# Two splits ahead of the last up block's evacuation, and a pair's sums due one weight later, in a hybrid encoder block

## The chip, the core and the metric

The kernel runs on one core of a Trainium2 chip. The metric is the device time of one execution, in microseconds (us); lower is better. Before the change it was 694.92 us, the median of three runs (694.84 to 695.49).

## What is computed

One layer of an encoder on 512 positions of width 1024, in float32. The part that matters here is the channel mixer at its end, FFN_HIDDEN = 2816 wide:

```python
h = rms_norm(x, norm_ffn_g[l])
up = causal_dwconv(h @ w_up[l], conv_ffn_w[l])
a, b = jnp.split(up, 2, axis=-1)
x = x + (jax.nn.silu(a) * b) @ w_down[l]
return rms_norm(x, norm_f_g)
```

The layer's first half (short convolution, forgetting attention, gates and merge) lies ahead of it and is not touched.

## The kernel before

**Layout.** Positions lie along the free axis, channels in 22 blocks of 128 on the partitions. Block j of the hidden layer has two column blocks of w_up, its a half (weight `up2j`) and its b half (`up2j+1`). The mixer has two phases (L43): blocks 0 to 11 with their share of w_down, then blocks 12 to 21 with the rest. A phase is an *up stage* followed by a *down stage*.

**Weights in two parts.** Every product is made from high and low parts: `wh*xh + wl*xh + wh*xl`, three float32r matmuls of 128x128 by 256 columns. So each weight that comes from memory is *split* before use (`split`, L253): ACT copies it into `wh` (L275), DVE subtracts that copy from the raw weight into `wl` (L279). `wh` and `wl` have two buffers each: a weight can be split once the weight two places before it is done on PE. A split also issues the load of a weight some places ahead on SP, and it then runs some of the planner's list (below).

**Seven products.** The down stages, and the up stages of blocks 1, 2, 5, 14 and 16 (`SUP`, L61), use a Strassen-like scheme: a two by two block product in seven products instead of eight (`seven`, L824). A step there has two weights, P (three products of each of two doubles: 18 matmuls) and F (four: 24 matmuls). An ordinary up weight has 48 matmuls. The names used below: the first down stage begins with P18, F18, P19, F19; block 14 uses P30, F30, P31, F31; the second down stage begins with P34, F34 and P35, and its fourth step is P37. Blocks 15, 17, 18, 19 and 20 have the weights up30/31, up34/35, up36/37, up38/39 and up40/41. Within a P or F all `wh` matmuls stand first, then those with `wl`; of an ordinary up weight the first eight matmuls use `wh` alone.

**Evacuation of an up block** (`up`, L1141). For each half: DVE multiplies the bank with the norm's scale (`mul`, L1171), ACT and DVE make the three taps of the convolution (`taps`: ACT L566, DVE L567 and L570). Behind the second half comes the gating (`glu`, L1227): ACT's SiLU (L1231; in the last block a table load for the coming square root, L1233, too) and a product of the halves. For an even j it is `ge` on GpSimd (POOL, L1236), for an odd one `go` (L1243). Two gated blocks form a pair q = j // 2: their *sums* are four short DVE steps (t13 in L1253 and L1254, t24 in L1257 and L1258), and the values and sums are split like weights into `gh` (ACT, L1262) and `gl` (DVE, L1263), in four steps.

**The planner.** What isn't urgent goes into the list `later` as (due, cost, tags, function). `run_later` (L224) runs, at each split, what is due by that weight's number while a budget of microseconds lasts: 4.2 for an up weight, 1.6 for a P and 1.2 for an F while anything tagged "e" (an evacuation) is pending, and 1.7, 1.6 and 0.75 otherwise (L286, L288). It skips what is not due and stops at the first due step that doesn't fit. Steps run in this way are queued behind the split's own copy and subtraction on their engines (`after_split`, L159). A pair's sums and splits are put in front of the "e" steps. After a seven-product block, its merge (nine steps) is tagged "e", and the evacuations of the blocks behind it are tagged so as well until the list is empty of them; otherwise an evacuation is issued at once. `glu` of an odd block first runs all that is left of earlier pairs (`flush_only`, L1238), because `go` has one buffer.

A pair's dues count from k, the number of the weight last split when `glu` runs: L1268.

```python
d = (2, 3, 4) if j + 1 < PHASES[ph][1] else (4, 5, 6)
```

The sums are due at k + d[0], two of the four splits at k + d[1] and two at k + d[2]. For the last block of a phase `go` itself is put off too, to k + 3, on DVE.

**Order on the engines.** PE's order is the code's. On ACT and DVE the tile framework, when it builds the program, puts the instructions in an order by its own estimate of when each is ready; among ready ones the code's order decides. The order that it chose is what the trace shows.

Of the kernel before, what the change touches and what calls it, by code (L numbers as in the profile page):

```python
# [42 lines left out]
PHASES = ((0, 12), (12, NP))  # L43
# [17 lines left out]
SUP = ((1, 2, 5), (14, 16))  # L61
# [9 lines left out]
def block_kernel(ctx, tc, xT, vecs, wv, win, wmix, wo, wup, wst, wdp, outT):  # L71
# [10 lines left out]
    def keep(ins):  # L82
        return tc.keep_in_program_order(ins)
# [72 lines left out]
    later = []  # L156
    held = dict.fromkeys(NRAW, 0)

    def after_split():  # L159

        st = ExitStack()
        for ins in order.values():
            st.enter_context(tc.issue_after(ins))
        return st

    def tag_of(k):
        return "raw" if stream[k][0][0] != "F" else "rf" if k >= ff0 else "rg"

    def load(upto):
        for k in range(len(raws), min(upto, len(stream) - 1) + 1):  # L170
            nm, src, ncol = stream[k]
            tag = tag_of(k)
            if held[tag] == NRAW[tag] or tag not in pools:
                return
            held[tag] += 1
            raw = pools[tag].tile([P, D], F32, tag=tag, name=f"raw_{nm}", bufs=NRAW[tag])
            if k == 0:

                keep(nc.scalar.dma_start(raw[:, VB:ncol], src[:, VB:]))
                keep(nc.sync.dma_start(raw[:, :VB], src[:, :VB]))  # L180
            else:
                keep(nc.sync.dma_start(raw[:, :ncol], src if tag == "raw" else made[src]))
            raws.append(raw[:, :ncol])
# [40 lines left out]
    def run_later(k, us):  # L224

        n = 0
        while n < len(later):
            if later[n][0] <= k and later[n][1] <= us + 0.1:
                us -= later[n][1]
                with after_split():  # L230
                    later.pop(n)[3]()
            elif later[n][0] <= k:
                return
            else:
                n += 1
# [11 lines left out]
    def flush_only(tags):  # L247

        while n := [n for n, w in enumerate(later) if set(w[2]) & set(tags)]:
            with after_split():  # L250
                later.pop(n[0])[3]()

    def split(hl=None):  # L253

        k = len(parts)
        if k == len(stream):
            return
        nm, _, ncol = stream[k]
        load(k + (LOOK if len(raws) > KB else AHEAD))
        if hl is None:  # L260
            hl = []
            for x in "hl":
                if k == 0:
                    wp.tile([P, PADW[x]], F32, tag=f"pad{x}", name=f"pad_{x}")
                w0 = VOFF if k < KB else 0
                hl.append(wp.tile([P, D], F32R, tag=f"w{x}", name=f"w{x}_{nm}", bufs=2)[:, w0 : w0 + ncol])
        hi, lo = hl
        raw = raws[k]
        if k == 0:
            for cs in (slice(VB, S + H), slice(0, VB)):  # L270
                keep(nc.vector.tensor_copy(hi[:, cs], raw[:, cs]))
        elif k == 1:
            keep(nc.vector.tensor_copy(hi, raw))
        else:
            ins = nc.scalar.activation(hi, raw, AF.Copy)  # L275
            order["hi"] = ins.ins
            if k < KB:
                keep(ins)
        ins = nc.vector.tensor_sub(lo, raw, hi.bitcast(F32))  # L279
        order["lo"] = ins.ins  # L280
        if k < KB:
            keep(ins)
        held[tag_of(k)] -= 1
        parts.append((hi, lo))
        if any(("e",) in w[2] for w in later):
            run_later(k, {"u": 4.2, "P": 1.6, "F": 1.2}[nm[0]])  # L286
            return
        run_later(k, {"u": 1.7, "P": 1.6, "F": 0.75, "i": 3.0, "m": 3.0, "d": 0 if nm == "dp1" else 2.1}.get(nm[0], 3.5))  # L288
# [275 lines left out]
    def taps(u, z, w):  # L564

        nc.scalar.activation(u, z, AF.Copy, scale=col(w + 2))  # L566
        nc.vector.scalar_tensor_tensor(  # L567
            u[:, 1:], z[:, : S - 1], col(w + 1), u[:, 1:], op0=ALU.mult, op1=ALU.add
        )
        nc.vector.scalar_tensor_tensor(  # L570
            u[:, 2:], z[:, : S - 2], col(w), u[:, 2:], op0=ALU.mult, op1=ALU.add
        )
# [117 lines left out]
    z, e, o = (ap.tile([n, S], F32, tag="pp", name=nm, bufs=NPP) for nm in ("fz", "fe", "fo"))  # L690
# [104 lines left out]
    for i in range(n + LA):  # L795
# [8 lines left out]
        if 0 <= i - LA < n:  # L804
            pr, e, qb = units[i - LA]
# [335 lines left out]
    def up(j, ph, rb2, pu=None):  # L1141
        uu = []

        def tap(i, z):
            u = fp.tile([P, S], F32, tag="fu", name=f"fu{j}{i}", bufs=3)
            taps(u, z, CF + 3 * (2 * j + i))
            uu.append(u)

        if j in SUP[ph]:
            c = 2 * SUP[ph].index(j)  # L1150
            slot()
            seven(
                UPD[ph][c : c + 2], NU[ph] + c, {j: USETS[j]}, lambda q, g: up_form(ph, q, g), of="x",
                done=lambda i, banks, ids: merge(ph, j, banks, ids, rb2, tap, uu),
            )
            slot()
            return
        evacs = []
        for i in range(2):
            slot()  # L1160
            p = pu[i] if pu else block(f"up{2 * j + i}", x1h, x1l, True)
            if i and j + 1 == PHASES[ph][1]:
                split_next()
                if any(("e",) in w[2] for w in later):
                    flush_only((("e",),))
                    split()
            z = [None]

            def mul(i=i, p=p, z=z):
                z[0] = fp.tile([P, S], F32, tag="fz", name=f"fz{j}{i}", bufs=4)  # L1170
                nc.vector.tensor_mul(z[0], p, rb2)  # L1171

            evac = [(0.7, mul), (1.4, lambda i=i, z=z: tap(i, z[0]))]
            if i:
                evac.append((0, lambda: glu(ph, j, uu)))
            if any(("e",) in w[2] for w in later):
                later.extend((0, us, (("e",), acc.last) if x == 0 else (("e",),), f) for x, (us, f) in enumerate(evac))
            else:
                for _, f in evac:
                    f()  # L1180
# [46 lines left out]
    def glu(ph, j, uu):  # L1227
        a, b = uu
        q, k = j // 2, len(parts) - 1
        g0 = place(ph, q)  # L1230
        nc.scalar.activation(a, a, AF.Silu)  # L1231
        if j == NP - 1:
            nc.scalar.activation(tbl, a[: 4 * H, :1], AF.Sqrt, scale=0.0, bias=eps[: 4 * H])  # L1233
        if j % 2 == 0:
            ge = glu.even = fp.tile([P, 2, 2 * P], F32, tag="ge", name=f"ge{q}", bufs=2)
            keep(nc.gpsimd.tensor_mul(ge, a.rearrange(halves_of, h=2), b.rearrange(halves_of, h=2)))  # L1236
            return
        flush_only([("q", x) for x in range(q)])  # L1238
        ge = glu.even
        go = fp.tile([P, 6, 2 * P], F32, tag="gr", name=f"go{q}")  # L1240

        def mul(eng):
            return eng.tensor_mul(go[:, 0:2, :], a.rearrange(halves_of, h=2), b.rearrange(halves_of, h=2))  # L1243

        if j + 1 < PHASES[ph][1]:
            keep(mul(nc.gpsimd))
        else:
            later.append((k + 3, 0.7, (("q", q),), lambda: mul(nc.vector)))
        b11, b12 = ge[:, 0, :], ge[:, 1, :]
        b21, b22, t1, t2, t3, t4 = (go[:, i, :] for i in range(6))  # L1250

        def t13():
            nc.vector.tensor_sub(t1, b11, b12)  # L1253
            nc.vector.tensor_sub(t3, b22, b12)  # L1254

        def t24():
            nc.vector.scalar_tensor_tensor(t2, t1, -1.0, b22, op0=ALU.mult, op1=ALU.subtract)  # L1257
            nc.vector.scalar_tensor_tensor(t4, t2, -1.0, b21, op0=ALU.mult, op1=ALU.subtract)  # L1258

        def hl(src, gs):  # L1260
            def f():
                nc.scalar.activation(gh[:, gs, :], src, AF.Copy)  # L1262
                nc.vector.tensor_sub(gl[:, gs, :], src, gh.bitcast(F32)[:, gs, :])  # L1263

            return f


        d = (2, 3, 4) if j + 1 < PHASES[ph][1] else (4, 5, 6)  # L1268
        w = [(d[0], 0.85, t13), (d[0], 0.85, t24), (d[1], 0.7, hl(ge[:, : 1 + ph, :], slice(g0, g0 + 1 + NF * ph, NF)))]
        w += [(d[x > 0 and 2 or 1], 0.7, hl(go[:, x : x + 2, :], slice(g0 + 1 + x, g0 + 3 + x))) for x in (0, 4, 2)]  # L1270
        at = next((x for x, i in enumerate(later) if ("e",) in i[2]), len(later))
        later[at:at] = [(k + n, us, (("q", q),), f) for n, us, f in w]
# [264 lines left out]
```

## Time and profile before

| | |
|---|---|
| median of three runs | 694.92 us |
| profiled execution | 694.18 us |
| its span, first to last instruction | 692.4 us |
| granted TensorE clock, mean | 0.997 |
| ACT busy | 53% |
| POOL busy | 28% |
| largest wait of ACT's weight copies for PE, in total (wh_F) | 28.7 us |

Rows of the timeline are read so: start in us from the first instruction, duration in us, engine, line of the code, operation, out<-in by the program's names (numbers left out, so `wh_F` is the high part of any F weight), shapes, and a count where equal instructions follow each other; in brackets the time that the engine stood idle just before, and what ended it. PE's matmuls overlap, so their starts, not their ends, show its pace. Rows of the waits: engine, line, "<-" what it waited for, total us, times, longest.

### The profile page before, as it was taken

The page shows a single profiled execution, that of the slowest core. Times are in us where ns is not written, and L with a number is a line of the kernel's source. Part 1 is how long each engine was busy: PE and PEld are TensorE (multiplying, and loading weights), DVE is VectorE, ACT ScalarE, POOL GpSimd, SP SyncE. Part 2 cuts the span into 40 slices and gives each one's busy share as a digit, 9 for nine tenths or more (in the row PEclk, how much of TensorE's full clock was granted, in tenths as well). Part 3 has the DMA queues.
Part 4 walks back from the last instruction along what each step waited for, and adds up shares of the span by engine and source line. Part 5 has one row for each costly group of instructions (what it writes and reads, how often), then busy time and mean ns, then how long its engine had stood idle before and what let it go on. Part 6 is the DMA issues. An engine that isn't in the chain of part 4 may idle for free. (4 is left out here: it accounts for less than half of the span.)

```text
span 692.4 us, 14690 instructions
## 1 busy us (share of the span) xinstructions
PE 683.1 (99%) x5936; PEld 680.6 (98%) x5936; DVE 554.2 (80%) x858; ACT 368.3 (53%) x579; POOL 190.5 (28%) x201
## 2 busy tenths in 40 slices
PE   9999999999999999999999999999999999999996
PEld 9999999999999999999999999999999999999995
DVE  6677787877578778769879699998787899988894
ACT  5675755554554444546554555545444544545572
POOL 6134947542020201214400144340100325231000
PEclk9999999999999999999999999999999999999998
DMA  8629999552568586788998498888945996676413
GB/s 308 225 67 293 216 243 204 134 120 92 185 144 221 166 268 205 230 308 213 158 313 241 126 233 222 200 242 231 252 149 167 337 231 157 188 168 182 154 31 122
DMA packets 65012, 137.53 MB, mean 199 GB/s; under 512 B 5760, under 2 KB 30352, under 8 KB 64688
## 3 DMA queue, kind: packets, MB, share of 16 engines
q1 hardware_dynamic: 44664, 107.28, 47.2%
q0 software_dynamic: 18464, 26.03, 23.4%
q10 hardware_dynamic: 1816, 3.29, 1.3%
q8 instruction: 46, 0.75, 0.4%
q14 instruction: 22, 0.18, 0.1%
HBM read 132.31 MB, written 47.71 MB: 260 GB/s over the span
## 5 line engine op out<-in xcount | busy, mean ns | idle before, releaser
L211 POOL DMA_DIRECT2D f<-in_wst_dram x66 | 77.7, 1371 | 27.1 <-DMA f<-f 26.8
L309 PE MATMUL p_up<-x1h,wh_up 128*128 128x256 f32 x416 | 81.2, 276 | 0.0
L309 PE MATMUL p_up<-x1l,wh_up 128*128 128x256 f32 x416 | 81.0, 276 | 0.0
L309 PE MATMUL p_up<-x1h,wl_up 128*128 128x256 f32 x416 | 81.0, 276 | 0.0
L279 DVE TENSOR_TENSOR wl_F<-raw_F,wh_F 128x1024 fp32r<-128x1024 f32 (+1 forms) x42 | 55.9, 1330 | 20.0 <-ACT wh_F L275 20.0
L275 ACT ACTIVATE wh_F<-raw_F 128x1024 fp32r<-128x1024 f32 (+1 forms) x42 | 44.3, 1054 | 39.5 <-PE dn L327 28.7
L309 PEld LDWEIGHTS p_up<-x1h,wh_up 128*128 128x128 f32 x416 | 62.7, 188 | 0.0
L309 PEld LDWEIGHTS p_up<-x1l,wh_up 128*128 128x128 f32 x416 | 62.7, 188 | 0.0
L309 PEld LDWEIGHTS p_up<-x1h,wl_up 128*128 128x128 f32 x416 | 62.6, 188 | 0.0
L309 PE MATMUL p_in<-xgh,wh_in 128*128 128x256 f32 x288 | 56.8, 279 | 0.0
L309 PE MATMUL p_in<-xgh,wl_in 128*128 128x256 f32 x288 | 56.6, 278 | 0.0
L309 PE MATMUL p_in<-xgl,wh_in 128*128 128x256 f32 x288 | 56.5, 278 | 0.0
L279 DVE TENSOR_TENSOR wl_P<-raw_P,wh_P 128x768 fp32r<-128x768 f32 (+1 forms) x42 | 41.7, 992 | 14.7 <-ACT wh_P L275 8.6
L327 PE MATMUL dn<-gh,wh_F 128*128 128x256 f32 x216 | 51.2, 277 | 1.2 <-ACT wh_F L275 1.2
L275 ACT ACTIVATE wh_P<-raw_P 128x768 fp32r<-128x768 f32 (+1 forms) x42 | 35.1, 835 | 32.1 <-PE dn L327 23.2
L327 PE MATMUL dn<-gl,wh_F 128*128 128x256 f32 x216 | 51.0, 276 | 0.0
L1236 POOL TENSOR_TENSOR ge<-fu,fu 128x512 f32<-128x512 f32 x11 | 20.1, 1831 | 110.5 <-DVE fu L570 85.6
L279 DVE TENSOR_TENSOR wl_up<-raw_up,wh_up 128x1024 fp32r<-128x1024 f32 x34 | 43.8, 1288 | 7.4 <-ACT wh_up L275 7.4
L275 ACT ACTIVATE wh_up<-raw_up 128x1024 fp32r<-128x1024 f32 x34 | 35.8, 1054 | 19.4 <-PE p_up L309 9.3
L309 PEld LDWEIGHTS p_in<-xgh,wh_in 128*128 128x128 f32 x288 | 44.7, 188 | 0.7
L309 PEld LDWEIGHTS p_in<-xgl,wh_in 128*128 128x128 f32 x288 | 43.7, 188 | 0.0
L309 PEld LDWEIGHTS p_in<-xgh,wl_in 128*128 128x128 f32 x288 | 43.6, 188 | 0.0
(343 smaller groups left out, 2211.8 us busy)
## 6 DMA issues: line engine op xcount, KB each, us to landing
raw_F<-f SPq DMA_DIRECT2D x41, 512.0 KB, 5.7
raw_up<-in_wup_dram SPq DMA_DIRECT2D x34, 512.0 KB, 5.6
raw_P<-in_wst_dram SPq DMA_DIRECT2D x41, 384.0 KB, 5.4
raw_in<-in_win_dram SPq DMA_DIRECT2D x24, 512.0 KB, 3.6
f<-in_wst_dram POOLq DMA_DIRECT2D x41, 256.0 KB, 6.8
f<-in_wst_dram SPq DMA_DIRECT2D x20, 512.0 KB, 7.1
f<-in_wst_dram POOLq DMA_DIRECT2D x20, 512.0 KB, 9.1
f<-f SPq DMA_DIRECT2D x40, 256.0 KB, 6.5
```

The source lines that it names most:

```text
L211: return lambda: keep(nc.gpsimd.dma_start(dst, src, accum_op=ALU.add))
L275: ins = nc.scalar.activation(hi, raw, AF.Copy)
L279: ins = nc.vector.tensor_sub(lo, raw, hi.bitcast(F32))
L309: keep(nc.tensor.matmul(out[:, cs], w, x[:, cs], start=start and i == 0 and c == 0, stop=stop and i == 2 and c == len(cut) - 1,))
L327: keep(nc.tensor.matmul(out, wl if x == 1 else wh, xl if x == 2 else xh, start=opens and bk not in seen, stop=closes and bk not in left,))
L1236: keep(nc.gpsimd.tensor_mul(ge, a.rearrange(halves_of, h=2), b.rearrange(halves_of, h=2)))
```

## The change

In `up`, for the second half of the last block of a phase: before, one split followed by a second one only if an "e" step is pending, in which case these are run first. After, two splits in any case, and then the pending "e" steps. In `glu`, the dues of a pair whose next block is one of `SUP` (j = 1, 13 and 15) go from (2, 3, 4) to (3, 4, 5).

```diff
             if i and j + 1 == PHASES[ph][1]:
                 split_next()
-                if any(("e",) in w[2] for w in later):
-                    flush_only((("e",),))
-                    split()
+                split()
+                flush_only((("e",),))
...
-        d = (2, 3, 4) if j + 1 < PHASES[ph][1] else (4, 5, 6)
+        d = (4, 5, 6) if j + 1 == PHASES[ph][1] else (3, 4, 5) if j + 1 in SUP[ph] else (2, 3, 4)
```

Since the second split comes ahead of the last block's `glu`, k is one larger there, and with it the dues of that pair (q5 in the first phase, q10 in the second).

## The prediction

> **What bounds the kernel now.** I read the page's first lines, then the waits of PE, then PE's timeline around each wait.
>
> ```profile
> span 692.4 us, 14690 instructions
> PE 683.1 (99%) x5936; PEld 680.6 (98%) x5936; DVE 554.2 (80%) x858; ACT 368.3 (53%) x579; POOL 190.5 (28%) x201
> ```
>
> PE is the bound, so an edit counts only if it shortens or makes a hole in PE's row. The waits of PE name weight splits alone:
>
> ```profile
> PE dn L327 <- ACT wh_F L275: 1.2, 2, 0.7
> PE dn L327 <- DVE wl_F L279: 0.4, 1, 0.4
> ```
>
> The timeline shows four holes in the channel mixer:
>
> ```profile
> 467.13 0.84 PE L327 MATMUL dn<-gh,wl_P 128*128 128x256 f32 x6
> 468.62 0.38 PE L327 MATMUL dn<-gh,wh_F 128*128 128x256 f32 x1 [0.66 <-ACT wh_F L275]
> ```
>
> ```profile
> 554.09 0.28 PE L327 MATMUL dn<-gl,wh_F 128*128 128x256 f32 x1
> 554.72 0.38 PE L327 MATMUL dn<-x1h,wl_F 128*128 128x256 f32 x1 [0.35 <-DVE wl_F L279]
> ```
>
> ```profile
> 609.59 0.28 PE L327 MATMUL p_up<-x1l,wh_up 128*128 128x256 f32 x1
> 610.02 0.50 PE L327 MATMUL p_up<-x1h,wl_up 128*128 128x256 f32 x2 [0.15 <-DVE wl_up L279]
> ```
>
> ```profile
> 632.55 0.73 PE L327 MATMUL dn<-gh,wl_P 128*128 128x256 f32 x5
> 633.78 0.38 PE L327 MATMUL dn<-gh,wh_F 128*128 128x256 f32 x1 [0.50 <-ACT wh_F L275]
> ```
>
> Six matmuls last 0.84 us with the last one's 0.28, so starts are 0.113 us apart ((0.84 - 0.28) / 5). The last of the six starts at 467.70; the next at 468.62, 0.81 late, and the one after a hole starts a further 0.11 late. Counted so, the holes are 0.92 (F18, first down stage), 0.63 (F31, beside the pair of block 13), 0.43 (up40) and 0.78 (F34, second down stage): 2.76 us, 0.4% of the span. This is all that the change can win.
>
> **The splits in front of the last evacuation.** At line 1164 nothing tagged "e" is pending in either phase: the merges' items are used up some weights earlier. So before makes one split there, the change two. No instruction is added; the second split (one ACT copy, one DVE subtraction, one load on SP) is traced ahead of the evacuation of the last block. What waits there?
>
> ```profile
> 464.44 1.66 ACT L1262 ACTIVATE gh<-go 128x512 fp32r<-128x512 f32 x3
> 466.99 0.63 ACT L1231 ACTIVATE fu<-fu 128x512 f32<-128x512 f32 x1 [0.89 <-DVE fu L570]
> 467.53 1.04 ACT L275 ACTIVATE wh_F<-raw_F 128x1024 fp32r<-128x1024 f32 x1
> ```
>
> ```profile
> 630.54 0.63 ACT L1231 ACTIVATE fu<-fu 128x512 f32<-128x512 f32 x1 [2.15 <-DVE fu L570]
> 631.19 1.28 ACT L1233 ACT_TABLE_LOAD   x1
> ```
>
> ```profile
> 632.69 1.04 ACT L275 ACTIVATE wh_F<-raw_F 128x1024 fp32r<-128x1024 f32 x1
> ```
>
> ACT's copy for F stands behind the SiLU, and the SiLU waits for DVE's taps of the *first* block of the pair. Moving the split ahead in the code should cure this. But the engines' order is not the code's: of the three copies at 464.44 the code issues two behind this SiLU (L1238's flush). The program is put in order by what is expected to be ready, the code's order deciding only among ready ones. The SiLU needs the first block's taps; the split needs the weight buffer that the *last* block frees at its end. So the SiLU, and in phase 1 the table load, can still go first, and I take **0 gained** at F18 and F34. The other end is both holes, 1.70 us.
>
> The move has a second effect. The new split runs what is due (L288), here one of the two q4 pairs that before flushes in L1238; it and the other one are now queued behind F18's own split on both engines.
>
> ```profile
> 466.82 1.28 DVE L1263 TENSOR_TENSOR gl<-go,gh 128x512 fp32r<-128x512 f32 x2
> 468.02 0.68 DVE L1171 TENSOR_TENSOR fz<-p_up,rb_n 128x512 f32<-128x512 f32 x1
> 468.63 1.21 DVE L279 TENSOR_TENSOR wl_F<-raw_F,wh_F 128x1024 fp32r<-128x1024 f32 x1
> 469.76 0.74 DVE L567 SCALAR_TENSOR_TENSOR fu<-fz,vec,fu 128x511 f32<-128x511 f32 x1
> 470.42 0.95 DVE L279 TENSOR_TENSOR wl_P<-raw_P,wh_P 128x768 fp32r<-128x768 f32 x1
> ```
>
> ```profile
> 472.83 0.39 PE L327 MATMUL dn<-gh,wl_P 128*128 128x256 f32 x2
> ```
>
> Before, DVE used its wait for F18's copy for these two (1.20 us). Now it idles there and does them from 469.76 on: 0.60 each, taps 0.66 each, so P19's subtraction starts at 469.76 + 2 x 0.60 + 2 x 0.66 = 472.28 and ends at 473.23. PE wants it at 472.83: a new hole of 0.40, plus 0.06 to start (554.72 against 553.44 + 1.22 = 554.66) and 0.11 behind it, less rounding: **+0.55**. If the split slips in ahead of the second tap, as at 470.42, it is 0. The later dues of q5 and q10 move one weight too; at P37 their last pair lands within 0.1 us of its use, which I take as 0, up to 0.2. The load on SP waits for its buffer as before: 0; its cover is the seven weights that loads run ahead (L253), and without that a load on SP would show among PE's waits, which name no DMA.
>
> **The sums one weight later.** It touches blocks 1, 13 and 15. At block 1:
>
> ```profile
> 392.26 1.22 DVE L279 TENSOR_TENSOR wl_F<-raw_F,wh_F 128x1024 fp32r<-128x1024 f32 x1 [3.28 <-ACT wh_F L275]
> ```
>
> DVE stands idle for 3.28 us four weights behind that pair, more than the four sums and two pairs that are moved toward it (2.54 us by the prices below), so 0; were that idle time gone, they would press on one weight's subtraction at most. At block 13:
>
> ```profile
> 549.64 1.07 ACT L275 ACTIVATE wh_F<-raw_F 128x1024 fp32r<-128x1024 f32 x1 [0.92 <-PE dn L327]
> ```
>
> ```profile
> 551.82 0.43 DVE L1254 TENSOR_TENSOR go<-go,ge 128x256 f32<-128x256 f32 x1 [1.19 <-POOL go L1243]
> ```
>
> ```profile
> 553.44 1.22 DVE L279 TENSOR_TENSOR wl_F<-raw_F,wh_F 128x1024 fp32r<-128x1024 f32 x1
> ```
>
> DVE stands for 1.19 us at a sum that needs POOL's product, with F31's subtraction behind it, whose copy is ready at 550.71. One weight later the sum is queued behind P31 rather than F30 and the split can pass: **-0.63**. What is late next is up30's subtraction; it comes earlier too, since the 1.19 us that stood ahead of both are gone.
>
> At block 15 the planner's arithmetic changes more than the due. Split of up36 has 4.2 us to give. Before: the two sums (1.7), one product (0.7), one tap pair (1.4). With the sums not due, it takes both products and both tap pairs, 0.7 + 1.4 + 0.7 + 1.4 = 4.2, and then block 17's gating, whose L1238 flushes **all** of q7 at once: four sums and four subtractions. All are traced ahead of up37's split.
>
> ```profile
> 584.22 1.22 DVE L279 TENSOR_TENSOR wl_up<-raw_up,wh_up 128x1024 fp32r<-128x1024 f32 x1
> 585.36 0.42 DVE L1253 TENSOR_TENSOR go<-ge 128x256 f32<-128x256 f32 x1
> ...
> 586.36 0.68 DVE L1171 TENSOR_TENSOR fz<-p_up,rb_n 128x512 f32<-128x512 f32 x1
> 586.97 0.92 DVE L1258 SCALAR_TENSOR_TENSOR go<-go 128x256 f32<-128x256 f32 x1
> ...
> 589.30 1.22 DVE L279 TENSOR_TENSOR wl_up<-raw_up,wh_up 128x1024 fp32r<-128x1024 f32 x1
> ...
> 596.50 1.77 DVE L567 SCALAR_TENSOR_TENSOR fu<-fz,vec,fu 128x511 f32<-128x511 f32 x1
> ```
>
> ```profile
> 593.39 0.62 PE L327 MATMUL p_up<-x1h,wl_up 128*128 128x256 f32 x4
> ```
>
> ```profile
> 584.45 3.16 POOL L1236 TENSOR_TENSOR ge<-fu,fu 128x512 f32<-128x512 f32 x1 [2.50 <-ACT fu L1231]
> ```
>
> ```profile
> 595.59 2.14 POOL L1243 TENSOR_TENSOR go<-fu,fu 128x512 f32<-128x512 f32 x1 [6.12 <-ACT fu L566]
> ```
>
> From 585.36, behind up36's subtraction: two products (0.60), four tap steps (0.66), four sums (1.00 / 3 from 585.36 to 586.36, so 0.33), four subtractions (0.60): 1.20 + 2.64 + 1.34 + 2.40 = 7.58; POOL's product at 584.45 costs one DVE step 0.50 (0.92 against 0.42). Up37's subtraction starts at 593.44 instead of 589.30 and ends at 594.66; PE wants it at 593.39: **+1.38** with the 0.11 behind it. Lower bound: it passes the last tap and pair (1.26 less), 0.1. Upper: POOL's next product falls on it, +1.03 (1.77 against 0.74 at 596.50), 2.4.
>
> The Trainium skill (SBUF — State Buffer, "SBUF: two separate sides") says that VectorE, reading two SBUF inputs, and GpSimd take their shared ports as a lock and the loser blocks. By that, up37's subtraction would stand for up to POOL's whole instruction. The stretched rows at 586.97 and 596.50 agree, each beside a POOL product.
>
> In return block 17 is through a weight earlier, q8's sums move from up39 to up38, and two instead of four subtractions stand in front of up40's split: 1.20 us fewer, where DVE was 0.32 late (610.02 against 609.59 + 0.11). Its hole goes: **-0.43**; it stays, 0, if DVE is still behind from up37.
>
> **Sum:** -0.63 - 0.43 + 0.55 + 1.38 = +0.87 us. The profiled execution took 694.18 with a span of 692.4; the median shown is 694.92. Added to the median: **695.8**.
>
> **Rivals.** *The list passes* (chance 0.17): up37's subtraction goes ahead and only gains remain, -1.06 to -0.5: 693.9 to 694.4. For it: at 470.42 a split did slip between two taps. Against: the sums and pairs are traced ahead of it and all ready.
> *The splits do what they say* (0.15): ACT copies F before SiLU and table load, 1.70 more and no hole at P19: 0.87 - 1.70 - 0.55 = -1.38, 693.5; with the list passing too, 692.2. Against: the copies at 464.44.
> *POOL falls on the split* (0.28), slower: block 17's product starts when the last q7 subtraction has freed its tile, about when up37's split starts. It costs 1.03 more, 696.9; it decides as soon as it adds over 0.5 us to the +0.87. For it: the two stretched rows. Against: at 586.97 the step hit came 2.5 us after POOL's start.
> *As forecast* (0.40).
>
> **How the numbers follow.** A measurement of this kernel can tell about 0.2%, 1.39 us, from no change. The forecast and *the list passes* lie within; *POOL* is slower but for a part (0.25 of 0.28, and 0.07 of the forecast's own spread with the holes at P19 and P37 large); *the splits* are faster. So faster 0.15, same 0.53, slower 0.32. The range, 693.4 to 697.1, takes in the splits' 693.5 and *POOL's* 696.9 with P37's 0.2; the forecast's own is 695.0 to 696.4.
>
> **What would show it.** Right: the holes at F18 and F34 stand, with SiLU ahead of the copy on ACT; that at F31 is gone; a new one of 1 to 2.4 us in up37, with eight q7 steps ahead of its subtraction on DVE; up40 runs through; P19 waits about half a microsecond for DVE. Wrong: a copy of F ahead of its SiLU, or up37 without a wait.

## The result and the profile after

The change takes 698.27 us (median of six runs, 697.78 to 700.1); the kernel before, in the same rounds, 694.90 (694.32 to 695.49). The ratio is 1.0051 with a 95% interval of 1.0039 to 1.0063: 2.7 to 4.4 us slower. The forecast was 695.8 with a range up to 697.1.

The first lines of the page of the change:

```profile
span 696.0 us, 14691 instructions
## 1 busy us (share of the span) xinstructions
PE 683.1 (98%) x5936; PEld 681.0 (98%) x5936; DVE 554.4 (80%) x858; ACT 368.3 (53%) x579; POOL 187.5 (27%) x201
```

PE's busy time is that of before to the tenth, so the 3.6 us more of span are time in which PE stands still, between its matmuls or behind the last of them. What PE waits for (total, times, longest; the line numbers of the change are one lower than before's from L1166 on):

```profile
PE p_up L327 <- DVE wl_up L279: 1.5, 1, 1.5
PE dn L327 <- DVE gl L1262: 1.4, 1, 1.4
...
PE dn L327 <- ACT wh_F L275: 0.6, 1, 0.6
PE dn L327 <- DVE wl_P L279: 0.3, 1, 0.3
```

The second row is new in kind: before, no row of PE named `gl`, the low part of the gated values. The rows of PE's timeline that belong to these waits:

```profile
467.00 0.84 PE L327 MATMUL dn<-gh,wl_P 128*128 128x256 f32 x6
468.48 0.38 PE L327 MATMUL dn<-gh,wh_F 128*128 128x256 f32 x1 [0.64 <-ACT wh_F L275]
...
473.13 0.98 PE L327 MATMUL dn<-gh,wl_P 128*128 128x256 f32 x6 [0.28 <-DVE wl_P L279]
```

```profile
594.83 0.74 PE L327 MATMUL p_up<-x1h,wl_up 128*128 128x256 f32 x4 [1.45 <-DVE wl_up L279]
```

```profile
649.32 0.39 PE L327 MATMUL dn<-gl,wh_P 128*128 128x256 f32 x1 [1.36 <-DVE gl L1262]
```

Counted as in the prediction, from start to start less 0.113 us and with the 0.11 behind each hole, the four are 0.91 (F18), 0.56 (P19), 1.73 (up37) and 1.74 us (P37). F31, up40 and F34 run through. The holes of the channel mixer are 4.94 us instead of 2.75 (2.76 in the prediction, by rounding): **+2.19**. Where each comes from:

**F18 and P19.** ACT and DVE there:

```profile
466.85 0.63 ACT L1230 ACTIVATE fu<-fu 128x512 f32<-128x512 f32 x1 [1.94 <-DVE fu L570]
467.38 1.04 ACT L275 ACTIVATE wh_F<-raw_F 128x1024 fp32r<-128x1024 f32 x1
...
469.60 0.68 DVE L1262 TENSOR_TENSOR gl<-go,gh 128x512 fp32r<-128x512 f32 x1
470.20 0.74 DVE L567 SCALAR_TENSOR_TENSOR fu<-fz,vec,fu 128x511 f32<-128x511 f32 x1
...
470.86 0.68 DVE L1262 TENSOR_TENSOR gl<-go,gh 128x512 fp32r<-128x512 f32 x1
471.47 0.74 DVE L570 SCALAR_TENSOR_TENSOR fu<-fz,vec,fu 128x510 f32<-128x510 f32 x1
472.13 0.95 DVE L279 TENSOR_TENSOR wl_P<-raw_P,wh_P 128x768 fp32r<-128x768 f32 x1
```

The SiLU still goes ahead of F's copy, though the code now has the copy first. The two `gl` of q4 stand between F18's subtraction and P19's, which starts at 472.13.

**Up37.** DVE behind up36's subtraction, and POOL's product:

```profile
584.33 1.22 DVE L279 TENSOR_TENSOR wl_up<-raw_up,wh_up 128x1024 fp32r<-128x1024 f32 x1
...
586.06 0.92 DVE L1252 TENSOR_TENSOR go<-ge 128x256 f32<-128x256 f32 x1
...
592.30 0.68 DVE L1262 TENSOR_TENSOR gl<-go,gh 128x512 fp32r<-128x512 f32 x1
592.90 0.74 DVE L570 SCALAR_TENSOR_TENSOR fu<-fz,vec,fu 128x510 f32<-128x510 f32 x1
593.56 1.21 DVE L279 TENSOR_TENSOR wl_up<-raw_up,wh_up 128x1024 fp32r<-128x1024 f32 x1
593.79 2.15 POOL L1242 TENSOR_TENSOR go<-fu,fu 128x512 f32<-128x512 f32 x1 [6.32 <-DVE fu L570]
594.70 0.68 DVE L1170 TENSOR_TENSOR fz<-p_up,rb_n 128x512 f32<-128x512 f32 x1
595.30 1.72 DVE L279 TENSOR_TENSOR wl_up<-raw_up,wh_up 128x1024 fp32r<-128x1024 f32 x1
```

All eight q7 steps lie between 586.06 and 592.98; up37's subtraction starts at 593.56, 4.26 us later than before. POOL's product for block 17 starts 0.23 us behind it and does not lengthen it (1.21 us); it lengthens that of up38 (1.72).

**F34.** ACT there, and PE's last products of P34:

```profile
630.27 0.63 ACT L1230 ACTIVATE fu<-fu 128x512 f32<-128x512 f32 x1 [1.92 <-DVE fu L570]
630.92 1.28 ACT L1232 ACT_TABLE_LOAD   x1
...
632.41 1.05 ACT L275 ACTIVATE wh_F<-raw_F 128x1024 fp32r<-128x1024 f32 x1
...
633.49 0.84 PE L327 MATMUL dn<-gh,wl_P 128*128 128x256 f32 x6
```

The order is that of before, SiLU, table load, copy. But PE's last P34 product starts at 633.49 + 5 x 0.113 = 634.06 instead of 633.01, and by then the copy, done at 633.46, is in time.

**P37.** ACT and DVE ahead of PE's 649.32:

```profile
645.91 0.41 DVE L1257 SCALAR_TENSOR_TENSOR go<-go 128x256 f32<-128x256 f32 x1
645.96 1.05 ACT L275 ACTIVATE wh_F<-raw_F 128x1024 fp32r<-128x1024 f32 x1
646.24 1.28 DVE L1262 TENSOR_TENSOR gl<-go,gh 128x512 fp32r<-128x512 f32 x2
646.91 0.61 ACT L1261 ACTIVATE gh<-go 128x512 fp32r<-128x512 f32 x1
647.45 1.22 DVE L279 TENSOR_TENSOR wl_F<-raw_F,wh_F 128x1024 fp32r<-128x1024 f32 x1
648.58 0.68 DVE L1262 TENSOR_TENSOR gl<-go,gh 128x512 fp32r<-128x512 f32 x1
```

Before, the last three of q10's four subtractions stood in one row, ahead of F37's:

```profile
644.70 1.89 DVE L1263 TENSOR_TENSOR gl<-go,gh 128x512 fp32r<-128x512 f32 x3
646.54 1.23 DVE L279 TENSOR_TENSOR wl_F<-raw_F,wh_F 128x1024 fp32r<-128x1024 f32 x1
```

In the change three of the four are done at 647.5. The fourth needs the last sum (645.91) and ACT's copy of it, which is queued behind the copy for F37 and ends at 647.52. F37's subtraction took the place ahead of it: 1.22 us, while PE waits. PE wants the fourth at 647.7; without F37's subtraction ahead of it, by estimate, it would have ended at 647.45 + 0.68 = 648.13, still late.

**Behind PE's end.** From the start of the last output step on DVE to the end of the span the change takes 696.0 - 688.08 = 7.9 us, before 692.4 - 685.84 = 6.6:

```profile
685.84 2.54 DVE L1412 TENSOR_TENSOR xm<-xm,pb_n 128x256 f32<-128x256 f32 x5 [0.80 <-PE pb_n L363]
```

```profile
688.08 2.54 DVE L1411 TENSOR_TENSOR xm<-xm,pb_n 128x256 f32<-128x256 f32 x5 [0.80 <-PE pb_n L363]
```

The DMA view of the 5.9 us from there on, its GB/s in 40 slices and its queues, first before, then the change:

```profile
GB/s 0 0 0 0 0 0 0 0 56 375 361 98 0 236 396 382 389 375 382 382 396 375 375 389 389 389 382 368 396 216 63 0 0 0 0 0 0 0 0 0
...
q14 instruction: 1, 0.01, 0.3%
```

```profile
GB/s 0 0 0 0 0 0 0 0 49 361 375 105 0 229 375 403 368 389 375 396 382 396 236 146 368 396 396 354 354 361 209 21 28 21 49 14 21 28 21 0
...
q14 instruction: 2, 0.02, 1.5%
```

The same stores move at the same rate, but in the change a thin rest of some 24 GB/s, a sixteenth of the full rate of 380, runs on for 1.2 us, as if one of the 16 DMA engines were late. Counted from the start of the last output step, the last store lands at 5.8 us in the change and at 4.5 before; in both the span ends some 2.1 us after that. Two fetches of engine code of 8 KB took 1.5% of 16 x 5.9 us = 1.4 us there, against 0.3 us for one before.

So the theory so far: +2.19 us of holes, each with its own cause, and some tenths of a us to 1.4 behind PE's end.

### The profile page after: what moved, and what is told of

Read it like the earlier page. It is cut to its first block, busy times and chain, and to the rows that moved or that the text cites. A ratio compares the mean times of both kernels' runs of the same rounds, so it can differ in the third digit from the quotient of the medians.

```text
span 696.0 us, 14691 instructions
## 1 busy us (share of the span) xinstructions
PE 683.1 (98%) x5936; PEld 681.0 (98%) x5936; DVE 554.4 (80%) x858; ACT 368.3 (53%) x579; POOL 187.5 (27%) x201
## 5 line engine op out<-in xcount | busy, mean ns | idle before, releaser
L279 DVE TENSOR_TENSOR wl_up<-raw_up,wh_up 128x1024 fp32r<-128x1024 f32 x34 | 45.8, 1347 | 5.1 <-ACT wh_up L275 5.0
L1235 POOL TENSOR_TENSOR ge<-fu,fu 128x512 f32<-128x512 f32 x11 | 17.8, 1620 | 110.4 <-DVE fu L570 94.8
```

## The experiments

Holes in us on PE, counted as above; "end" runs from the start of the last output step to the end of the span; the ratio is that to the kernel before in the same rounds.

| kernel | F18 | P19 | F31 | up37 | up40 | F34 | P37 | sum | end | ratio (95%) |
|---|---|---|---|---|---|---|---|---|---|---|
| before | 0.92 | | 0.63 | | 0.43 | 0.77 | | 2.75 | 6.6 | |
| change | 0.91 | 0.56 | | 1.73 | | | 1.74 | 4.94 | 7.9 | 1.0051 (1.0039 to 1.0063) |
| e1 | 0.94 | 0.42 | 0.89 | | 0.72 | 0.79 | 1.74 | 5.50 | 7.2 | 1.0041 (1.0028 to 1.0054) |
| e2 | 0.94 | | | 1.45 | | | | 2.39 | 7.2 | 0.9999 (0.9990 to 1.0008) |
| e3 | 0.94 | | | | 0.43 | 0.80 | | 2.17 | 7.4 | 0.9987 (0.9978 to 0.9996) |
| e4 | 0.93 | 0.56 | | 1.73 | | | | 3.22 | 7.4 | 1.0012 (1.0003 to 1.0021) |
| e5 | 0.94 | 0.57 | | 1.73 | | | 1.74 | 4.98 | 7.8 | 1.0036 (1.0024 to 1.0048) |
| e6 | 0.94 | 0.57 | | | 0.84 | 0.86 | 1.74 | 4.95 | 7.2 | 1.0032 (1.0020 to 1.0043) |
| e7 | 0.94 | 0.57 | | 1.73 | | | 0.73 | 3.97 | 7.1 | 1.0021 (1.0012 to 1.0030) |
| e8 | 0.39 | | | | 0.44 | | | 0.83 | 7.6 | 0.9964 (0.9952 to 0.9976) |
| e9 | | | | | | | | 0 | 7.0 | 0.9962 (0.9949 to 0.9975) |
| e10 | 0.94 | | 0.62 | | 0.73 | 0.81 | | 3.10 | 7.7 | 1.0015 (1.0005 to 1.0024) |
| e11 | 0.94 | 0.56 | | 1.47 | | | 1.74 | 4.71 | 6.6 | 1.0018 (1.0010 to 1.0027) |
| e12 | 0.94 | | 0.62 | | 0.44 | 0.78 | | 2.78 | 7.7 | 1.0001 (0.9993 to 1.0010) |
| e13 | 0.94 | | 0.62 | | 0.45 | 0.81 | | 2.82 | 6.5 | 0.9995 (0.9986 to 1.0004) |
| e14 | | | | | | | | 0 | 6.6 | 0.9946 (0.9933 to 0.9958) |

Span less holes less end is 683.1 to 684.3 us in all sixteen executions: the two columns "sum" and "end" carry the differences, up to some 0.6 us either way. Part of this rest arises at the start: the fiftieth matmul, 9 us into the span, comes within a range of 0.9 us from one execution to another.

**e1, the splits alone.** The new lines at 1163 to 1165, with the old dues.

> The two splits ahead of the last evacuation alone, all dues of blocks 1, 13 and 15 as before. Theory (each part makes its own holes): P19 waits 0.56 us and P37 1.74 us for DVE, because q5's and q10's dues move one weight; F31 (0.63) and up40 (0.43) stay; F18 stays at 0.9, and F34 stays at about 0.8, since the split does not by itself pass the SiLU and the table load. Holes +2.3 us on before: 697.2 with the end of before (6.6 us behind the last output step's start), 698.6 if the end is 1.4 us longer as after. Rival A (P37's hole is what DVE's backlog from up37 leaves): no hole at P37, 0.2 at most; 695.4. Rival B (the split does cure F34): F34's hole is gone, 0.8 us less than the theory, 696.4 to 697.8.

Measured 698.06 us (before 695.38). The two PE rows that decide, in e1:

```profile
635.01 0.39 PE L327 MATMUL dn<-gh,wh_F 128*128 128x256 f32 x1 [0.52 <-ACT wh_F L275]
```

```profile
650.28 0.39 PE L327 MATMUL dn<-gl,wh_P 128*128 128x256 f32 x1 [1.36 <-DVE gl L1262]
```

P37's hole is there in full with up37 running through, so rival A falls; F34's stands at 0.79 with both splits in front, so rival B falls. P19's 0.42, F31's 0.89 and up40's 0.72 are not what was expected. As far as the medians tell, all of the change's loss is in this part.

**e2, the dues alone.**

> The dues of blocks 1, 13 and 15 one weight later alone, the splits as before. Theory: up37 waits 1.73 us, the holes of F31 (0.63) and up40 (0.43) are gone, no hole at P19 and P37; F34's hole (0.78) is gone too, because PE comes there about 0.7 us later than before and the same chain on ACT is then in time: -0.1 us, 694.8, with the end of before. Rival A (P37's hole is DVE's backlog from up37): a hole of 1.7 us at P37, 696.5. Rival B (F34 was cured by the split): F34's hole stands at 0.8, 695.6.

Measured 695.17 (before 695.38). Up37 waits, 1.45 rather than 1.73; F31, up40 and F34 run through, P19 and P37 too. F34's hole is thus gone without the splits, wherever up37 has made PE late, and stays with them where it hasn't (e1, and e6 below).

**e3, the due of block 13 alone.**

```diff
-        d = (2, 3, 4) if j + 1 < PHASES[ph][1] else (4, 5, 6)
+        d = (4, 5, 6) if j + 1 == PHASES[ph][1] else (3, 4, 5) if j == 13 else (2, 3, 4)
```

> Only the dues of block 13 one weight later. Theory: F31's hole of 0.63 us goes and nothing else moves: holes of 2.1 us in all, 694.3. Rival (the order of the whole program changes with any due): new holes elsewhere in the second phase, 694.9 or more.

Measured 694.59 (before 695.38): 0.3 to 1.5 us faster by its interval. F31's hole went, and nothing took its place.

**e4, the change with the last pairs' dues set back.** The put-off product at k + 2 instead of k + 3, d = (3, 4, 5) instead of (4, 5, 6).

> The change, but the dues of the last pair of a phase (q5, q10) and the put-off product set back by one, so that they fall on the same weights as before. Theory: P37's hole of 1.74 us goes, that of P19 (q4's pairs behind F18's split, which the dues of q5 don't touch) stays at 0.56, up37 stays at 1.73, F34 stays gone: 1.7 us less than the change, 696.5 with the change's end, 695.2 with that of before. Rival (DVE is late at P37 from up37's backlog, or the split of F37 is put first whatever the dues): P37's hole stays, 698.3.

Measured 696.29. P37 runs through, all other holes are those of the change. So P37's hole comes from k being one larger in `glu`, not from the place of the split.

**e5, the change once more.**

> The change itself once more. Its holes on PE are 2.2 us more than before's, but its median was 3.4 us higher; in its profiled execution the last 1.4 us lay behind PE's end (7.9 us from the start of the last output step to the end of the span, 6.6 before, 7.2 to 7.4 in the first four experiments), where two code fetches of 8 KB ran beside the last stores. Theory 1 (the length of the end belongs to the program, which has one ACT and two DVE instructions more): again 7.9, and the median 3.4 us above before. Theory 2 (chance of the execution): an end of 6.6 to 7.4, and a median 2.2 to 2.9 us above before.

Measured 698.24, 2.5 us above before (695.74). The holes repeat within 0.04. The end is long again (7.8), as theory 1 said; the median lies where theory 2 put it. Undecided by this run alone.

**e6, 4.0 us for up36.**

```diff
-            run_later(k, {"u": 4.2, "P": 1.6, "F": 1.2}[nm[0]])
+            run_later(k, {"u": 4.0 if nm == "up36" else 4.2, "P": 1.6, "F": 1.2}[nm[0]])
```

> The change with 4.0 us instead of 4.2 to give at up36's split, so that the second tap pair and block 17's gating don't fit there any more. Theory (the planner's sum of exactly 4.2 put block 17's gating and the flush of all eight q7 steps in front of up37's subtraction): up37's hole of 1.73 us goes. PE is then earlier at F34, and its hole of 0.8 us comes back; up40's of 0.4 may. So 0.5 to 0.9 us less than the change, P37's 1.74 and P19's 0.56 unchanged. Rival (DVE is that far behind whatever the list does, or POOL's product falls on up37's subtraction): a hole of over 0.5 us stays in up37.

Measured 697.78, 0.46 less than e5, which the two intervals don't tell from nothing. Up37 runs through: the planner's sum of exactly 4.2 was its cause. But the 1.73 us come back as 0.84 at up40 and 0.86 at F34; the holes are what they were (4.95 against 4.98), and the gain that was expected doesn't show in them. Up37's hole had been paying for two others.

**e7, q10's subtractions ahead of F37's.** F37's subtraction is queued on DVE behind the four `gl` of q10.

```diff
+        with ExitStack() as st:
+            for g in last_gl if nm == "F37" else ():
+                st.enter_context(tc.issue_after(g))
-        ins = nc.vector.tensor_sub(lo, raw, hi.bitcast(F32))
+            ins = nc.vector.tensor_sub(lo, raw, hi.bitcast(F32))
```

> The change, with F37's subtraction put in DVE's queue behind the four subtractions of q10. Theory (at P37 the order decides: F37's subtraction of 1.22 us stands ahead of the one subtraction of q10 that waits for its last sum): the hole falls from 1.74 us to about 0.6, what DVE is late by with that step in first place (647.45 + 0.68 = 648.13 against 647.68, with 0.11 behind it), and F37 doesn't wait. 1.1 us less than the change. Rival (the dues moved alone are the cause, the order nothing): the hole stays over 1.4, since the sums end too late.

Measured 696.83, 1.4 less than e5; the holes give 1.0 of it. DVE and PE at P37, in e7:

```profile
647.03 2.01 DVE L1265 TENSOR_TENSOR gl<-go,gh 128x512 fp32r<-128x512 f32 x3
648.96 1.22 DVE L282 TENSOR_TENSOR wl_F<-raw_F,wh_F 128x1024 fp32r<-128x1024 f32 x1
```

```profile
649.10 0.39 PE L330 MATMUL dn<-gl,wh_P 128*128 128x256 f32 x1 [0.34 <-DVE gl L1265]
```

The hole falls from 1.74 to 0.73: 1.0 us of it is the order of two instructions. The other 0.7 stays in the order of the code: with the later dues DVE and ACT come to the fourth subtraction too late for PE. Why the framework put F37's subtraction first is not in the trace.

**e8, ACT's copies first.** Two splits, the earlier pairs' steps flushed between them; the SiLU (first phase) and the table load (second) are queued behind F's copy; the last pairs' dues as in e4; otherwise only block 13's due is later.

```diff
                 split_next()
+                flush_only([("q", x) for x in range(j // 2)])
                 split()
...
+        with tc.issue_after(order["hi"]) if j + 1 == PHASES[0][1] else ExitStack():
-        nc.scalar.activation(a, a, AF.Silu)
+            nc.scalar.activation(a, a, AF.Silu)
...
+            with tc.issue_after(order["hi"]):
-            nc.scalar.activation(tbl, a[: 4 * H, :1], AF.Sqrt, scale=0.0, bias=eps[: 4 * H])
+                nc.scalar.activation(tbl, a[: 4 * H, :1], AF.Sqrt, scale=0.0, bias=eps[: 4 * H])
```

> Two splits ahead of the last evacuation, but the earlier pairs' steps issued between them; ACT's copy of F18 queued ahead of the SiLU, that of F34 ahead of the table load; the last pairs' dues on the same weights as before; of the other dues only block 13's one later. Theory: F18's 0.92, F34's 0.78 and F31's 0.63 go, none comes at P19, P37 and up37; up40's 0.43 stays: 2.3 us less than before, 692.6. Rival A (the copies can't be earlier, as the buffer comes free too late): F18 and F34 keep over 0.5 each, 693.8 or more. Rival B (what is queued behind the copies, the gating and the taps, is late in turn): new holes of 0.5 us or more at P19 to P37, 693.5 or more.

Measured 693.29 (before 695.74): 1.7 to 3.3 us faster. ACT's copies for F18 and F34, in e8:

```profile
466.53 1.07 ACT L275 ACTIVATE wh_F<-raw_F 128x1024 fp32r<-128x1024 f32 x1
...
629.99 0.63 ACT L1232 ACTIVATE fu<-fu 128x512 f32<-128x512 f32 x1 [2.15 <-DVE fu L570]
630.65 1.06 ACT L275 ACTIVATE wh_F<-raw_F 128x1024 fp32r<-128x1024 f32 x1
```

F18's copy starts at 466.53 instead of 467.53, F34's at 630.65 instead of 632.69, and PE waits for neither. In the second phase the SiLU still goes first; it was the table load that had to give way. F18 keeps 0.39, now for DVE's low part, which stands behind the scaling of the last block's second half.

**e9, cured.** On e8: that scaling is queued behind F's subtraction, and block 17's pair is due at (1, 2, 3).

> The last experiment (copies of F18 and F34 ahead of SiLU and table load) with two more orders: the scaling of the last block's second half queued behind the subtraction of F's low part on DVE, and the sums and values of block 17's pair due one weight earlier. Theory: the 0.39 us that F18 still waits for DVE goes, and up40's 0.44, since four sums and two subtractions of q8 no longer stand ahead of its subtraction: no hole over 0.1 us is left in the second half, 3 us less than before by the holes (2.76 plus rounding), 0.8 less than the last experiment: about 692.3 where before takes 695.0. Rival (DVE is full there, and what is taken from up40 is late at up39 or at P35): a hole of 0.4 us or more elsewhere, no faster than the last experiment.

Measured 692.69 (before 695.35): 1.7 to 3.5 us faster. The 0.8 us beyond e8 don't show in the medians, whose ratios are 0.9962 and 0.9964. None of the seven holes is left (a gap of 0.2 to 0.3 us ahead of P40, which all these kernels have, isn't in the table); PE's rows of waits in e9 lie in the first part of the program alone:

```profile
PE pa L477 <- ACT xgh L458: 1.1, 1, 1.1
PE warm L115 <- DVE ones L107: 1.1, 1, 1.1
```

**e10, before with three tiny instructions.** In the middle of the program, where `pools["rf"]` is set, two memsets of 4 columns on DVE and one copy of 4 columns on ACT, kept in order.

```diff
     pools["rf"] = fp
+    pad = [fp.tile([P, 4], F32, tag=f"pd{e}", name=f"pd{e}") for e in "va"]
+    for _ in range(2):
+        keep(nc.vector.memset(pad[0], 0.0))
+    for _ in range(1):
+        keep(nc.scalar.activation(pad[1], vec[:, :4], AF.Copy))
```

> The kernel before with one tiny instruction more on ACT and two on DVE in the middle of the program, away from every hole, so that these two engines end on the same numbers as in the change (836 and 1090 instructions). Theory 1 (the end is longer because the code of ACT and DVE is then fetched in 8 KB blocks beside the last stores): two fetches 3 to 4 us behind the start of the last output step, an end of 7.4 to 7.9 us instead of 6.6, and 0.8 to 1.3 us more than before. Theory 2 (chance): no difference of the median by over 0.4 us.

Measured 696.53 (before 695.35): 0.3 to 1.7 us slower, with two fetches in the last 5.9 us and an end of 7.7. The DMA view there, in e10:

```profile
q14 instruction: 2, 0.02, 1.6%
```

PE's waits name none of the three instructions, so the slower median fits theory 1; but some 0.3 us of the difference may be up40's hole, 0.73 in this execution, and e12 leaves still less to the fetches.

**e11, the change with sixteen.** The same with eight and eight.

> The change with eight tiny instructions more on ACT and eight on DVE at the same place. Theory 1: the fetches move ahead of the last stores, the end falls from 7.8 to 7.9 us to about 6.6, and the change is only 2.2 to 2.5 us slower than before. Theory 2: an end anywhere from 6.6 to 7.9, the median as for the change, 2.5 to 3.4 us above before.

Measured 696.77, by its interval 0.7 to 1.9 us above before: less than either theory said. The GB/s row of e11 over the 5.9 us; no `q14` row stands below it:

```profile
GB/s 0 0 0 0 0 0 0 0 56 375 361 98 0 236 396 382 389 368 382 382 396 375 389 382 382 396 382 375 389 216 7 0 0 0 0 0 0 0 0 0
```

The fetches are gone from the last stores, the thin rest with them, and the end is 695.2 - 688.65 = 6.6 us, as theory 1 said. The holes are still those of the change, but for up37's 1.47 instead of 1.73.

**e12, before once more.**

> The kernel before once more, for a second profile of its end and as a measure of what these rounds can tell. Theory 1: an end of 6.6 us again, with one code fetch beside the last stores. Theory 2: anything from 6.6 to 7.9. The ratio to before is 1 within its interval by both.

Measured 695.44, as before. But its end was 7.7 us, with one fetch that took long:

```profile
q14 instruction: 1, 0.01, 1.3%
```

Here theory 1 falls as far as it said that before's end is 6.6: with one fetch among the last stores it is 6.6 or 7.7, by the execution (the fetch started among the stores here, and as they ended before). What decides between them isn't known. That bears on e10 too: its end is no longer than this one. Of the 1.1 us between the spans of e10 and e12, 0.3 are holes, 0.03 the end, and 0.4 arise in the first 10 us. So these two executions don't show that the second fetch is what makes e10 slower.

**e13 and e14, before and e9 with sixteen.**

> The kernel before with eight tiny instructions more on ACT and eight on DVE in the middle of the program, as in the padded change. Theory (before's end too is lengthened by the one fetch beside its last stores, in most executions): no fetch within 3 us of the last output step, an end of 6.6 us, a median 0.4 to 0.9 us below before; the padded change is then 1.7 to 2.2 us above this one, its holes alone. Rival (before's usual end is 6.6 us, and 7.7 is rare): the median of before within 0.2 us.

> The cured version with the same sixteen tiny instructions more. Theory: no fetch beside the last stores, an end of 6.6 instead of 7.0 us, and 0.4 us or more less than the cured version: 0.5% below before. Rival (the other instruction counts shift the order of the whole program, or another engine's fetch falls there): no gain on the cured version, 0.38% below before.

e13: 695.06 (before 695.41), an end of 6.5; 0.35 us less, which its interval (1.0 less to 0.3 more) does not tell from nothing. Against e13 the padded change is 696.77 - 695.06 = 1.7 us slower, each in its own rounds; the holes differ by 4.71 - 2.82 = 1.9. With the fetches out of the way on both sides, the holes are enough to account for the difference. e14: 691.80 (before 695.41), an end of 6.6, 2.9 to 4.7 us faster than before: the lowest median found, though its interval overlaps that of e9.

## Why the prediction was wrong

**What held.** In the mixer PE's row decided, and the steps that were worked out came as worked out. The holes at F18 (0.91, stands) and P19 (0.56 against 0.55) came, F31's (-0.63) and up40's (-0.43) went. On ACT the SiLU stays ahead of the copy, whatever the code's order; e8 shows that it was this order: with the copy ahead of the SiLU at F18 and of the table load at F34, PE no longer waits for ACT at either. For up37 it named the cause, the budget of exactly 4.2 us and the flush of eight steps, and e6 shows it. Its size was 1.73 instead of 1.38: up36's subtraction starts 0.11 later than before, PE comes to up37 0.18 earlier (593.10 + 0.11 = 593.21 against 593.39), and the 0.06 from a subtraction's end to PE's start, which the prediction counts at P19, is left out at up37. Up40's gain hung on the flush at up36, as the prediction has it: in e6, without it, the hole is back (0.84).

**Where it failed.** The step is the half sentence on P37: "at P37 their last pair lands within 0.1 us of its use, which I take as 0, up to 0.2". It measured 1.74 us, half of the whole loss. Two things in it failed. The lateness, for which the prediction shows no working, was not 0.1 us: with q10's four subtractions in the code's order (e7) the hole is still 0.73. And the step took it that this order stays. F37's subtraction of 1.22 us passes the fourth, which stands waiting for the last sum and its copy, and that adds 1.0 (1.74 against 0.73). The prediction states for ACT that the order goes by expected readiness and did not ask the same of DVE; that this rule is what put F37's subtraction first is inferred, since no trace shows what the framework expected. That the hole comes from the later dues is shown by e4 (dues back: 0), that the order makes most of it by e7. The upper bound of such a step is not 0.2 us but its lateness and the longest instruction that can pass.

**What was missed in the sum.** F34 was booked at 0 by its order, rightly, but its hole went all the same: up37's hole makes PE 1.05 us later there (634.06 against 633.01), while ACT's copy is done 0.27 us earlier than before (633.46 against 633.73). The holes are not independent terms; e6 gives up37's 1.73 back and gets 0.84 + 0.86 elsewhere. Terms as predicted, in us, with what came: -0.63 and -0.43 (the same), +0.55 (+0.56), +1.38 (+1.73), F34 0 (-0.78), P37 0 (+1.74): +2.19 instead of +0.87.

**Behind PE's end.** The prediction allowed for nothing there, and says "No instruction is added"; the built program has one instruction more on ACT and two on DVE, none of them counted as busy. The holes give 694.9 + 2.2 = 697.1, the edge of the range. The rest of the median is 0.3 to 1.2 us by the two comparisons of the change. The end can make up that much: it was 7.9 and 7.8 us in the change, 6.6 and 7.7 before. That fetches among the last stores lengthen it is shown by e11, e13 and e14, where they are moved away and the end is 6.5 to 6.6. How much of the rest the second fetch makes is not shown: before's own end varies (e12), and what it loses on average isn't settled (e13).

**The rivals.** *POOL falls on the split* gave 696.9, nearest in size, but that was chance, as it is not what happened: POOL's product started 0.23 us behind up37's subtraction and hit up38's. This agrees with the Trainium skill (SBUF — State Buffer, "SBUF: two separate sides"), by which the instruction that starts first holds the shared ports: the one that started ahead of POOL took 1.21 us, the one that started behind it 1.72. *The list passes* and *the splits do what they say* did not happen (up37 waits; the SiLU stays first).

**What stays open.** Up40's hole was 0.43 to 0.45 in five kernels and 0.72 to 0.84 in three, up37's 1.45 to 1.47 in two and 1.73 in four, F31's 0.89 in e1 and 0.62 or 0.63 elsewhere, P19's 0.42 in e1 and 0.56 or 0.57 elsewhere; what makes these differences of up to 0.4 us was not tried. Nor is it known what makes e10 slower than before.

## What to carry to other kernels

Where a framework orders each engine's queue by expected readiness, price a small lateness at itself and the longest instruction that can pass the late one, and fix the order explicitly (e7 to e9) rather than moving code. A hole in the bounding engine gives slack to everything behind it, so holes are summed in order of time, each with the lateness that the earlier ones leave. And where tenths of a per cent matter, compare the end of the program apart from its work: a few instructions more can move a code fetch into the last stores or out of them.

## What the runs showed of the hardware that was not expected

Engine code is fetched by DMA while the program runs: the page of before counts 46 fetches with 0.75 MB on queue q8 and 22 with 0.18 MB on q14. At the end of the program one fetch of 8 KB took 0.3 us behind the stores' rush (before) and 1.2 us in it (e12, 1.3% of 16 x 5.9 us). The last store landed 4.5 us behind the start of the last output step in the four executions without a fetch among the stores (e11, e13, e14, and before, whose fetch starts as the stores end), and at 4.9 to 5.8 us in the other twelve; in all sixteen the span ended 1.9 to 2.3 us later than that. So the end was 6.5 to 6.6 us without a fetch (three executions), 6.6 to 7.7 with one (seven), 7.0 to 7.9 with two (six, the change's at the upper end). The Trainium skill (Runtime: NRT & Kernel Launch, "Instruction fetch mechanics") has the code refilled in blocks of 16 KiB at a cost that is mostly hidden. The blocks on q8 have that size (0.75 MB for 46); those on q14 are half of it (0.18 MB for 22), and beside the last stores they aren't hidden.
